# Gradient along the rows on one core: part of one early load moved to a second queue, and the waits set by hand

## The chip, the core and the metric

One of the cores of a Trainium2 chip runs the kernel. The metric is device time in microseconds (us); the lower the better. The core has five engines that run side by side (TensorE, VectorE or DVE, ScalarE or ACT, GpSimd or POOL, SyncE or SP) and 16 DMA engines that move data between main memory (HBM) and the on-chip memory of 128 partitions. An engine starts a transfer by issuing it on its queue; the 16 DMA engines carry the packets.

## The reference

```python
def setup_inputs():
    return {"x": np.random.randn(8192, 8192).astype(np.float32)}

def reference(x):
    return np.gradient(x, axis=1)
```

For every row: inside, `out[j] = (x[j+1] - x[j-1]) / 2`; at the two ends, the plain difference of the two outermost values. 268.4 MB are read and as many written.

## The kernel before

The 8192 rows are cut into 32 tiles of 256 rows. A partition holds two neighbouring rows (`R = 2`), so a tile is 128 partitions x 16384 float32, that is 65536 bytes in each partition, contiguous in main memory. Tile `i` lives in slot `i % 3` (`NB = 3`) of the on-chip memory. A slot is 64 columns wider than a tile: the load writes at column 64, the results are written from column 0 on.

For each tile, in the loop over `i`:

- `load(i)` (line 52): one transfer from main memory to the slot, issued on SP's queue. It waits for the store of tile `i - 3`, which used the same slot.
- POOL takes the four end differences into the small array `ends` (line 74). It waits for the load.
- DVE does all the rest of the tile in one instruction, a custom operation that subtracts and halves (line 80). It waits for line 74.
- DVE, or POOL for `i % 5` in (1, 3) but for the last two tiles, copies the end values over the two seams of the result (line 91).
- `store(i)` (line 56): one transfer from the slot to main memory, also on SP's queue. It waits for line 91. For `i % 3 == 1` (but the last) the store is held: it is issued after the next tile's step on line 74, so once that tile has landed.

After the third tile of a round the loads of the next three tiles are issued. SP's queue so alternates: three loads, three stores, three loads, and so on, 64 transfers in all; the last round has tiles 30 and 31. The order is written by hand (`manual_schedule`). The dependencies are declared to the framework by `chain`, which names the steps that an instruction must wait for; the framework places the semaphores.

## Time and profile before

| what | us |
|---|---|
| median of 3 runs | 1247.15 (1247.09 to 1247.3) |
| the profiled execution | 1246.62 |
| its span | 1244.7 |
| DVE busy | 554.6 |
| line 80, one tile (mean of 32) | 17.224 |
| POOL busy | 8.8 |
| first load issued, after the span's start | 0.74 |
| load, from issue to landing (median) | 57.9 |
| store, from issue to landing (median) | 40.2 |

The span is what the profiler saw of the program on the core; the time of the execution is 1.9 us more. The queue that SP fills is called q1 in the profile, the one that brings instructions to the engines q14. A transfer's landing is its semaphore's last update: a transfer of 128 partitions sends one update from each of 16 DMA engines, and the landing records hold the 16 times. The packet records hold the start, the duration and the size of each packet that a DMA engine moved, without the engine's number. Instructions of the sequencer itself (issues, semaphores, branches) carry a q behind the engine: SPq.

### The profile page before, as it was taken

What the parts mean: (1) busy time and instruction counts of PE and PEld (TensorE: products, weight loads), DVE (VectorE), ACT (ScalarE), POOL (GpSimd) and SP (SyncE); (2) the same over time, 40 slices, a digit from 0 to 9 for tenths busy, and PEclk for the clock granted to TensorE, in tenths of its full rate; (3) what the DMA queues carried; (4) which work ended last, traced back from release to release, by engine and by line L of the source; (5) the groups of instructions that cost most, each with busy time, mean ns of one, the idle gap of its engine ahead of it and who ended that gap; (6) DMA issues with size and microseconds to landing.
All of it is one profiled execution on the core that took longest, in us unless ns stands there. A gap on an engine that the chain in (4) does not pass through costs nothing.

```text
span 1244.7 us, 237 instructions
## 1 busy us (share of the span) xinstructions
DVE 554.6 (45%) x52; POOL 8.8 (1%) x48
## 2 busy tenths in 40 slices
DVE  2850582079009702850582079009603840591082
POOL 0000000000000000000000000000000000000000
DMA  9999999999999999999999999999999999999999
GB/s 404 438 436 423 421 438 438 438 438 428 432 430 430 438 438 438 423 436 436 430 434 436 438 428 432 438 436 434 425 436 434 432 436 436 436 434 430 434 409 404
DMA packets 9217, 536.88 MB, mean 431 GB/s; under 512 B 1024, under 2 KB 1024, under 8 KB 1024
## 3 DMA queue, kind: packets, MB, share of 16 engines
q1 hardware_dynamic: 9216, 536.88, 99.8%
q14 instruction: 1, 0.01, 0.0%
HBM read 268.44 MB, written 268.44 MB: 431 GB/s over the span
## 4 chain that ended last, share of the span: by engine, by line
another core or an unknown queue 74%; DVE 18%; DMA 3%; issue 2%; POOL 1%; SPq 0%; POOLq 0%
DVE slot L80 18%; DMA slot<-in_x_dram 3%; POOL ends L74 0%; POOL slot L91 0%; SPq L52 0%; POOLq L128 0%; DVE slot L91 0%
## 5 line engine op out<-in xcount | busy, mean ns | idle before, releaser
L80 DVE CUSTOM_DVE_ANT_0 slot<-slot 128x16382 f32<-128x16382 f32 x32 | 551.2, 17224 | 667.6 <-POOL ends L74 667.6
L74 POOL TENSOR_TENSOR ends<-slot 128x4 f32<-128x4 f32 x32 | 6.3, 198 | 988.5 <-DMA slot<-in_x_dram 988.5
L91 POOL COPY slot<-ends 128x4 f32<-128x4 f32 x12 | 2.3, 190 | 207.9 <-DVE slot L80 207.9
L91 DVE COPY slot<-ends 128x4 f32<-128x4 f32 x20 | 3.4, 172 | 0.7
L117 POOL MEMSET const-bfloat16-1.0<- 128x1 bf16 x1 | 0.1, 101 | 0.0
L117 POOL MEMSET const-uint8-127<- 128x1 uint8 x1 | 0.1, 101 | 0.0
L117 POOL MEMSET const-float32-0.0<- 128x1 f32 x1 | 0.1, 98 | 0.2 <-issue 0.2
L117 POOL MEMSET const-float32-1.0<- 128x1 f32 x1 | 0.1, 98 | 0.0
## 6 DMA issues: line engine op xcount, KB each, us to landing
slot<-in_x_dram SPq DMA_DIRECT2D x32, 57.9
out_dram<-slot SPq DMA_DIRECT2D x32, 40.2
```

What stands on the lines that cost most here:

```text
L74: ins = nc.gpsimd.tensor_sub(out=ends[:, i, :, :], in0=xin[:, :, 1 : m : m - 2], in1=xin[:, :, 0 : m - 1 : m - 2],)
L80: ins = nc.vector._custom_dve(dve_ops.TENSOR_TENSOR_REDUCE_SUB_MAX, out=b[:, 1 : W - 1], in0=b[:, SH + 2 : SH + W], in1=b[:, SH : SH + W - 2],
L91: ins = placer.tensor_copy(out=res[:, :, 0 : m : m - 1], in_=ends[:, i, :, :])
L117: nc = _bacc.Bacc("TRN2", target_bir_lowering=False, num_devices=1)
```

## The change

The last 960 of tile 2's 16384 columns (3840 of 65536 bytes in each partition) are no longer in SP's load of this tile. They are loaded by 15 transfers on ACT's queue, which the kernel did not use: of 15 partitions, of 14, and so on down to 2, and one of 9, from partition 127 downwards; together 128. All other loads and all stores are as before.

For this the framework's dependencies are given up: the whole loop stands in a critical section, and semaphores are allocated and waited for by hand. `landed[k]` counts 16 for each transfer into slot `k`, so tile 2 waits for 16 transfers; `stored[k]` counts the stores from the slot; `taken`, `halved` and `placed` count the three compute steps. At the end SP waits for the last store from each slot. The compute instructions, their engines and their order are the same, and so is SP's order of loads and stores.

```diff
+    SPLIT = 2
+    REST = 960
+    RANGES = (15, 14, 13, 12, 11, 10, 9, 8, 7, 6, 5, 4, 3, 2, 9)
...
-    def load(i):
-        b = slots[i % NB]
-        ins = nc.sync.dma_start(out=b[:, SH : SH + W], in_=x_sets[i])
-        loads.append(chain(i, ins, *([stores[i - NB]] if i >= NB else [])))
...
+    with tc.tile_critical():
+        landed = [tc.alloc_semaphore(f"landed{k}") for k in range(NB)]
...
+        def load(i):
+            k = i % NB
+            b = slots[k]
+            at = W - REST if i == SPLIT else W
+            if i >= NB:
+                nc.sync.wait_ge(stored[k], home[i - NB])
+            nc.sync.dma_start(out=b[:, SH : SH + at], in_=x_sets[i][:, 0:at]).then_inc(landed[k], 16)
+            n_landed[k] += 16
+            if i == SPLIT:
+                lo = P
+                for rows in RANGES:
+                    lo, hi = lo - rows, lo
+                    nc.scalar.dma_start(
+                        out=b[lo:hi, SH + at : SH + W], in_=x_sets[i][lo:hi, at:W]
+                    ).then_inc(landed[k], 16)
+                    n_landed[k] += 16
+            arrived[i] = n_landed[k]
...
+        def store(i):
+            k = i % NB
+            eng, count = done[i]
+            nc.sync.wait_ge(placed[eng], count)
+            nc.sync.dma_start(out=out_sets[i], in_=slots[k][:, 0:W]).then_inc(stored[k], 16)
+            n_stored[k] += 16
+            home[i] = n_stored[k]
...
+            nc.gpsimd.wait_ge(landed[k], arrived[i])
+            nc.gpsimd.tensor_sub(
...
+            ).then_inc(taken, 1)
+            nc.vector.wait_ge(taken, i + 1)
...
+            ).then_inc(halved, 1)
...
+            eng.wait_ge(halved, i + 1)
...
             if held is not None:
-                store(*held, at[0])
+                nc.sync.wait_ge(taken, i + 1)
+                store(held)
                 held = None
...
+        for k in range(NB):
+            nc.sync.wait_ge(stored[k], n_stored[k])
```

More of the change, by code (lines that the diff above doesn't have):

```diff
@@ L35 @@
     slots = [pool.tile([P, SH + W], f32, name=f"slot{k}", tag=f"slot{k}") for k in range(NB)]
-    loads, stores = [], [None] * nsets
-    in_front = {}
-    def chain(i, ins, *needed):
-        group, engine = f"slot{i % NB}", ins.ins.engine
-        keep = [o.ins for o in needed]
-        if in_front.get(engine, (None,))[0] == group:
-            keep.append(in_front[engine][1])
-        tc.declare_no_dep(ins.ins, group=group, keep=keep, reason="implied by the needed step")
-        tc.add_to_no_dep_group(group, ins.ins)
-        in_front[engine] = group, ins.ins
-        return ins
@@ L50, in load @@
-    def load(i):
-        b = slots[i % NB]
-        ins = nc.sync.dma_start(out=b[:, SH : SH + W], in_=x_sets[i])
-        loads.append(chain(i, ins, *([stores[i - NB]] if i >= NB else [])))
-    def store(i, done, later):
-        ins = nc.sync.dma_start(out=out_sets[i], in_=slots[i % NB][:, 0:W])
-        stores[i] = chain(i, ins, done)
-        if later is not None:
-            tc.add_manual_dep(
-                ins.ins,
-                later.ins.name,
-                mybir.DependencyInfo(mybir.DependencyClass.Sync, mybir.DependencyReason.DATA),
-                reason="issued once the next tile has landed",
-            )
@@ L66 @@
-    held = None
-    with tc.manual_schedule():
+    with tc.tile_critical():
+        landed = [tc.alloc_semaphore(f"landed{k}") for k in range(NB)]
+        stored = [tc.alloc_semaphore(f"stored{k}") for k in range(NB)]
+        taken = tc.alloc_semaphore("taken")
+        halved = tc.alloc_semaphore("halved")
+        placed = {nc.vector: tc.alloc_semaphore("placed_v"), nc.gpsimd: tc.alloc_semaphore("placed_g")}
+        n_landed, n_stored = [0] * NB, [0] * NB
+        n_placed = {nc.vector: 0, nc.gpsimd: 0}
+        arrived, home, done = [0] * nsets, [0] * nsets, [None] * nsets
+        def load(i):
[22 more added lines that the diff above has]
+            home[i] = n_stored[k]
@@ L68 @@
         for i in range(NB):
             load(i)
+        held = None
         for i in range(nsets):
-            b = slots[i % NB]
+            k = i % NB
+            b = slots[k]
             xin = b[:, SH : SH + W].rearrange("p (t m) -> p t m", m=m)
-            ins = nc.gpsimd.tensor_sub(
+            res = b[:, 0:W].rearrange("p (t m) -> p t m", m=m)
+            nc.gpsimd.wait_ge(landed[k], arrived[i])
+            nc.gpsimd.tensor_sub(
                 out=ends[:, i, :, :],
@@ L77 @@
                 in1=xin[:, :, 0 : m - 1 : m - 2],
-            )
-            at = [chain(i, ins, loads[i])]
-            ins = nc.vector._custom_dve(
+            ).then_inc(taken, 1)
+            nc.vector.wait_ge(taken, i + 1)
+            nc.vector._custom_dve(
                 dve_ops.TENSOR_TENSOR_REDUCE_SUB_MAX,
@@ L86 @@
                 s1=0.5,
-            )
-            halved = chain(i, ins, *at)
-            res = b[:, 0:W].rearrange("p (t m) -> p t m", m=m)
-            placer = nc.gpsimd if i % 5 in (1, 3) and i < nsets - 2 else nc.vector
-            ins = placer.tensor_copy(out=res[:, :, 0 : m : m - 1], in_=ends[:, i, :, :])
-            placed = chain(i, ins, halved)
+            ).then_inc(halved, 1)
+            eng = nc.gpsimd if i % 5 in (1, 3) and i < nsets - 2 else nc.vector
+            eng.wait_ge(halved, i + 1)
+            eng.tensor_copy(out=res[:, :, 0 : m : m - 1], in_=ends[:, i, :, :]).then_inc(placed[eng], 1)
+            n_placed[eng] += 1
+            done[i] = eng, n_placed[eng]
             if held is not None:
-                store(*held, at[0])
+                nc.sync.wait_ge(taken, i + 1)
+                store(held)
                 held = None
             if i % NB == 1 and i + 1 < nsets:
-                held = i, placed
+                held = i
             else:
-                store(i, placed, None)
+                store(i)
             if i % NB == NB - 1:
-                for k in range(i + 1, min(i + 1 + NB, nsets)):
-                    load(k)
+                for j in range(i + 1, min(i + 1 + NB, nsets)):
+                    load(j)
+        for k in range(NB):
+            nc.sync.wait_ge(stored[k], n_stored[k])
 _INS = ['x']
```

## The prediction

> **What bounds the kernel now.** I read the page first: what is busy, and the DMA queues.

> ```profile
> span 1244.7 us, 237 instructions
> ...
> DVE 554.6 (45%) x52; POOL 8.8 (1%) x48
> ...
> q1 hardware_dynamic: 9216, 536.88, 99.8%
> q14 instruction: 1, 0.01, 0.0%
> ...
> slot<-in_x_dram SPq DMA_DIRECT2D x32, 57.9
> out_dram<-slot SPq DMA_DIRECT2D x32, 40.2
> ```

> The compute engines are idle more than half the time; SP's queue q1 keeps the 16 DMA engines busy for 99.8% of the span. Next, the DMA share by stage (columns: stretch, its length, DVE busy, POOL busy, PE clock, DMA share, GB/s).

> ```profile
> 0.00:1.70 1.70, 0.00 (x0) 0.20 (x4) 1.00 0.00 0
> ...
> 62.00:1202.00 1140.00, 501.04 (x46) 7.83 (x40) 1.00 1.00 433
> 1202.00:1205.00 3.00, 1.54 (x2) 0.00 (x0) 1.00 0.87 371
> ```

> The queue never runs dry before 1202 us. The timeline shows why the 13% idle after it does not matter:

> ```profile
> 1185.91 0.20 POOL L74 TENSOR_TENSOR ends<-slot 128x4 f32<-128x4 f32 x1 [77.09 <-DMA slot<-in_x_dram]
> 1186.14 17.23 DVE L80 CUSTOM_DVE_ANT_0 slot<-slot 128x16382 f32<-128x16382 f32 x1 [59.86 <-POOL ends L74]
> 1203.40 0.17 DVE L91 COPY slot<-ends 128x4 f32<-128x4 f32 x1
> 1203.60 19.65 SPq L56 DMA_DIRECT2D out_dram<-slot  x2
> 1205.22 0.20 POOL L74 TENSOR_TENSOR ends<-slot 128x4 f32<-128x4 f32 x1 [19.11 <-DMA slot<-in_x_dram]
> ```

> Store 30 is issued at 1203.60 and its first packets start at 1204.5. The first DMA engine had finished load 31 at 1202.24 and waits; the last finished at 1205.15 and never waits. So the end is set by **the slowest of the 16 DMA engines**: its 512 packets, back to back.

> So I read the packet records one by one (start, duration, size). A packet is one row of 65536 bytes; it belongs to the engine whose packet before ended within 8 ns of its start. This gives 16 rows of 512 packets (one record is missing); the engines' numbers are not in the records. 7778 of 8192 packets take 2418 ns. I call "lag" how far an engine is behind an unbroken row of packets, 2.415 us apart, from 1.75 us on. Mean over the engines of what is added, in us:

> ```
> starts of the first packet (0 to 1.20 late)        0.25
> first packet longer than 2.418                      0.55
> tiles 0-1, rest                                     0.02
> load 2 (two thirds or more in its last packet)      1.16
> rounds 1-9, loads to stores: .06 .45 .07 .33 .21 .08 .35 .02 .02 = 1.59
> lag before store 30: mean 3.54, least 2.30, most 5.05
> ```

> The extra of a round sits almost wholly in the last load packet before the stores begin. The first time, at 58 us, all engines reach it within 0.65 us and lose 0.84 to 1.12 us each. The rounds that follow lose 0.06 to 0.45 while the engines are 0.6 to 2.0 us apart, and 0.02 once they are 2.6 us apart, which is more than one packet. The order is not smooth (.06 at 0.6 us apart), so this is a tendency, no law. Landings agree: 0.62 us between first and last engine at load 0, 2.92 at load 31.

> **The change, part by part.** The profiled execution took 1246.62 us (1.9 around its span), 0.53 under the median 1247.15; I add differences to the median.

> *Waits by hand.* Loads and stores keep their order on SP; POOL, DVE and the held stores wait for the same steps. One wait costs SP 17 ns (its EVENT_SEMAPHORE rows) and lies behind a full queue: nothing, up to 0.1 us at store 30 if it is exposed.

> *Entry and exit of the critical section.* Each engine gets one more branch, and SP a step in which it waits for the others and releases them. The trace has such handshakes at the end:

> ```profile
> L128 SPq EVENT_SEMAPHORE  x7: 17/28/28, 1223.3 to 1244.6; - x7
> L128 POOLq EVENT_SEMAPHORE  x4: 17/17/17, 1244.0 to 1244.6; - x4
> ```

> From the last landing, 1243.85, to 1244.67 there are two: about 0.4 each. One more before the first load and one after the last landing lie bare on the path: 2 x 0.35 = **+0.7** (0 if they share the old ones, 1.6 at twice that).

> *Fifteen issues on ACT.* SP's issue of a load takes 340 ns (median of 32); 15 make 5.1 us on an engine that does nothing else. Hidden: their data is wanted by tile 2, which lands at 62 us. If ACT held back SP's first load, the cost were one issue, 0.34. Tile 0 lands later by the pieces that slip in between its rows, 15 x 0.3 = 4.5 us at most; store 0 is then issued at 45 instead of 40.4, still ahead of its turn at 58.

> *Bytes moved between engines.* SP's load of tile 2 loses 3840 of 65536 bytes per row: 8 rows x 0.142 us (3840/65536 x 2.418) = 1.14 us less on every engine. The pieces come back on ACT's queue. How they spread is not in this trace: evenly would be 8 each and no shift. All on one engine is 128 x 0.151 = 19 us. I take one row an engine, counted from the same engine each time, since a row is the packet here. Then the fifteen transfers put 15 pieces on the first engine, 15, 14, 13 and so on, none on the last.

> [...]

> *Price of a piece.* Low end: 0.142 plus a 4-byte semaphore packet of 9 ns = 0.151. High end: the only packet of another ring under load (q14, 8192 bytes, 997.06 us) took 309 ns, and the q1 packet behind it on that engine 2579 instead of 2418, so 161 ns more: 0.312. That row is the nearest, but it came alone and unannounced, while the pieces stand queued; I take 0.205, a third of the way. The first engine then has 15 x 0.205 - 1.14 = **+1.94** (+1.13 to +3.54), the last -1.14.

> *What the shift does at the load-store turns.* The engines are now some 3.1 us apart (15 steps of 0.205) before the first turn, which the trace shows as nearly free (0.02). Of the 2.7 us lost from load 2 on I leave 0.9 for the slowest engine (0.2 if the turns are clean; all of it if spread is not the reason).

> Sum for the slowest: 0.25 + 0.55 + 0.05 + 1.94 + 0.9 = 3.7 against 5.05, so -1.35; with +0.7: -0.65, **1246.5 us**.

> **The rivals.**

> A, *faster*: clean turns and cheap pieces. 0.85 + 1.13 + 0.2 = 2.2, against 5.05: -2.85, handshakes +0.3: **1244.6**. For it: 15 steps of 0.151 fill 2.27 us, nearly one packet, so that one engine turns at a time. Against: rounds at 2.0 us apart still lost 0.35.

> B, *slower*: the switch between rings costs the full 161 ns each time. The first engine gets +3.54. Were its lag average before, it ends at 3.54 + 3.54 = 7.1, 2.0 past the old slowest, +0.7: **1249.9**; were it the slowest already, 1251.4. It decides once a piece costs over (5.05 - 3.54 + 1.14)/15 = 0.177 and the turns stay as dear. For it: the q14 row. Against: with spread the turns should get cheaper, which gives back up to 1.8.

> C, *only the handshakes*: the engines that get more bytes had slack (2.30 against 5.05), those that decide are little changed, the turns too: +0.7, **1247.9**. Against: the turns cost more than half the lag, and the shift reaches every engine before them.

> [...]

> D, *the pieces pile up* on one engine: +18 and more, **1265**.

> **How the numbers follow.** Forecast 0.42 (its own range 1245.2 to 1247.8), A 0.23, B 0.18, C 0.13, D and the unforeseen 0.04. A measurement of this kernel tells about 0.2%, 2.5 us: faster means under 1244.7, slower over 1249.6. A and a stray part of the forecast make faster 0.25; B and D 0.21; the rest, 0.54, is the same. Range 1244.2 to 1249.9: A's time with its bare handshakes, up to B's nearer end.

> **What would show it.** Entry: the first load's issue later than 0.74 us by some 0.35; exit: more than 0.82 us from last landing to end. Pieces: fifteen packets of 3840 bytes on one engine, fourteen on others, none on one, all before 40 us, and q1 packets of 2418 or some 2580 behind them. Turns: the packets at 58 us at 2.5 instead of 3.3 us. Spread at load 31 (2.92): about 3 if the shift stays, with the last landing of load 31 near 1204.5. I am wrong if the packets at 58 us stay at 3.3 though the engines are 2 us apart, or if pieces cost 0.3 and more.

## The result, and the profile after

The changed kernel takes 1249.61 us (median of 16 runs, 1248.88 to 1250.11), the kernel before 1247.12 (median of 16, 1246.46 to 1247.52): a ratio of 1.0020, interval 1.0013 to 1.0027. It is slower, by 2.5 us. The profiled execution took 1250.04 us, 3.42 more than that of before; 0.9 of this is that the one lies 0.43 above its median and the other 0.50 below, so the parts below are worth a little less in the median.

From the page of the changed kernel: the span, what is busy, the DMA queues. q10 is ACT's queue.

```profile
span 1248.1 us, 243 instructions
...
DVE 554.6 (44%) x52; POOL 8.8 (1%) x48
...
q1 hardware_dynamic: 9216, 536.38, 99.5%
q10 hardware_dynamic: 256, 0.49, 0.1%
q14 instruction: 1, 0.01, 0.0%
```

The engines do the same work, the DMA engines are as busy as before, and the same 537 MB are moved. The 256 packets of q10 are 128 pieces of 3840 bytes and 128 semaphore updates of 4 bytes. Now the start, in the timeline of the changed kernel (start, duration, engine, line, what; in brackets the idle time before it and what ended it).

```profile
0.91 6.08 ACTq L62 DMA_DIRECT2D slot<-in_x_dram  x15
0.95 1.33 SPq L56 DMA_DIRECT2D slot<-in_x_dram  x3
25.72 0.20 POOL L86 TENSOR_TENSOR ends<-slot 128x4 f32<-128x4 f32 x1 [25.28 <-DMA slot<-in_x_dram]
...
47.11 0.20 POOL L86 TENSOR_TENSOR ends<-slot 128x4 f32<-128x4 f32 x1 [21.20 <-DMA slot<-in_x_dram]
```

POOL's first step on a tile follows the tile's landing at once (tile 1 lands at 47.05, the step starts at 47.11). Here are the same two steps of the kernel before:

```profile
22.69 0.20 POOL L74 TENSOR_TENSOR ends<-slot 128x4 f32<-128x4 f32 x1 [22.25 <-DMA slot<-in_x_dram]
...
41.99 0.20 POOL L74 TENSOR_TENSOR ends<-slot 128x4 f32<-128x4 f32 x1 [19.10 <-DMA slot<-in_x_dram]
```

Tile 0 is there 3.0 us later, tile 1 5.1 us later. The view by stretches says where the bandwidth went (columns as before: stretch, length, DVE, POOL, PE clock, DMA share, GB/s). First the changed kernel, then the one before.

```profile
4.00:42.00 38.00, 16.05 (x1) 0.20 (x1) 1.00 0.99 396
```
```profile
4.00:42.00 38.00, 17.40 (x2) 0.21 (x2) 1.00 1.02 442
```

The DMA engines are busy all the time in both (share 0.99 and 1.02), and move a tenth less in the changed kernel (396 against 442 GB/s): the packets take longer. The packet records show which. These are the rows of the engine that carries no piece at all, start in us and duration in ns:

```
after, engine without pieces:  5.39 2434   7.82 2824   10.64 2714   13.35 3012   16.36 2418   18.77 2807   21.57 2418
                               23.99 2611  26.60 2702  29.30 2418   31.71 2666   34.38 2418   36.79 2682   39.47 2418
before, any engine:            2418 to 2420 for nearly every row of tiles 0 and 1 after the first
```

Its rows are stretched by 0.15 to 0.6 us whenever the others carry pieces, and take about 2418 in between. So the cost falls on all 16 engines, whoever carries the piece: of the 256 full rows that start before 45 us, 166 are stretched by more than 0.02 us, against 25 of 288 in the kernel before.

Why only every second row, the engine with all fifteen pieces shows (p is a piece, s its semaphore update of 4 bytes, K a row; start in us, duration in ns):

```
32.21:p149 32.35:K2651 35.00:s9 35.01:K2422 37.43:p149 37.57:K2675 40.24:s9 40.25:K2422 42.67:p149 42.81:K2805
```

A piece and its update each take a turn of their own between two rows. Fifteen pieces so stretch over some 28 rows: the last one starts at 67.60 us, where the prediction had all of them before 40 us, and POOL's step on tile 2 starts at 70.71 us instead of 62.37. The rows of SP's queue do not wait for that: store 0 still occupies the DMA engines then, and their share is 1.01 from 60 to 70 us and 0.99 from 70 to 90.

The end, from the sequencer's rows of the critical section (duration min/median/max, first and last start):

```profile
L40 SPq COMPARE_BRANCH  x1: 38/38/38, 1246.7 to 1246.7; - x1
...
L40 SPq NOP  x2: 13/16/18, 0.7 to 1247.2; - x2
```

The last store lands at 1246.26, SP leaves the section at 1246.7 and has all engines together at 1247.2; only then come the handshakes that the kernel before has too, up to 1248.05. From the last landing to the end it is 1.79 us, against 0.83.

The sum of the packets, in us and as a mean over the engines down to "all later extra" (the last landing is that of the slowest engine), with the prediction's way of counting (extra over 2.418 for 65536 bytes, in proportion for 61696):

```
                                before   after
first packet starts at            2.00    2.26
first row, extra                  0.55    0.18
rows of loads 0 to 2, extra       0.22    3.19
pieces, less the 1.14 saved          -    0.72
turn at 58 (61) us, extra         0.96    0.16
all later extra                   1.66    0.89
last landing                   1243.85 1246.26
from there to the end of the span 0.83    1.79
```

3.0 us are lost beside the pieces and 1.6 gained back at the turns; 0.7 is lost in the pieces themselves and 0.3 at the start, which the first row gives back. That is +2.0 in the mean (the landings of load 30 say +1.97), and the slowest engine now lies 2.20 behind the mean at load 30 (before: 1.70): +2.41 at the last landing. The section's exit adds 0.96.

### The profile page after: what moved, and what is told of

It reads as the page before. It is cut to its first block, busy times and chain, and to the rows that moved or that the text cites. A ratio compares the mean times of both kernels' runs of the same rounds, so it can differ in the third digit from the quotient of the medians.

```text
span 1248.1 us, 243 instructions
## 1 busy us (share of the span) xinstructions
DVE 554.6 (44%) x52; POOL 8.8 (1%) x48
## 2 busy tenths in 40 slices
DMA packets 9473, 536.88 MB, mean 430 GB/s; under 512 B 1152, under 2 KB 1152, under 8 KB 1280
## 3 DMA queue, kind: packets, MB, share of 16 engines
q1 hardware_dynamic: 9216, 536.38, 99.5%
## 4 chain that ended last, share of the span: by engine, by line
another core or an unknown queue 76%; DVE 18%; DMA 4%; POOL 1%; issue 0%; SPq 0%
DVE slot L92 18%; DMA slot<-in_x_dram 4%; POOL ends L86 1%; POOL slot L102 0%; SPq L56 0%; DVE slot L102 0%; SPq L143 0%; SPq L40 0%
## 6 DMA issues: line engine op xcount, KB each, us to landing
out_dram<-slot SPq DMA_DIRECT2D x32, 40.2
slot<-in_x_dram SPq DMA_DIRECT2D x31, 57.9
```

## The experiments

Each is a variation of the changed kernel or of the one before, run beside the kernel before on the same chip. Ratios are to that kernel. The table of the packets' extra follows after the last one.

### The section alone

```diff
-    REST = 960
-    RANGES = (15, 14, 13, 12, 11, 10, 9, 8, 7, 6, 5, 4, 3, 2, 9)
+    REST = 0
+    RANGES = ()
```

> The critical section with its hand-placed semaphores, but no pieces: tile 2 is loaded whole on SP's queue. Theory (the section's entry and exit cost 0.2 and 1.0 us, the pieces the rest): +1.2 us against the kernel before, packets of the first two loads at 2418 ns, the turn at 58 us at 3.3 us again. Rival (the section costs all of it): +2.5 us.

1248.27 us, ratio 1.0009 (1.0000 to 1.0018): +1.05 against 1247.22. The first load is issued at 0.95 instead of 0.74 us; from the last landing to the end it takes 1.69 us. Rows of tiles 0 and 1 keep 2418 ns, the turn costs 0.97 us. So the section explains 1.05 of the 2.5, and the pieces some 1.4.

### One transfer, evenly spread

```diff
-    RANGES = (15, 14, 13, 12, 11, 10, 9, 8, 7, 6, 5, 4, 3, 2, 9)
+    RANGES = (128,)
```

> The same 960 columns of tile 2 on ACT's queue, but as one transfer of 128 partitions: 8 pieces on every engine, no shift between engines. Theory R (a piece of another queue between SP's rows is what slows the rows): the rows of the first two loads are slow again, some 0.2 to 0.4 us for each round of pieces, 8 x 0.3 = 2.4 us, and +1.2 for the section, +3.6 us against before, and the turn at 58 us as dear as before. Theory F (a row is slowed because the pieces of 15 or fewer partitions are written to partitions that other engines write to): rows at 2418 ns, +1.2 us.

1248.29 us, ratio 1.0010 (1.0001 to 1.0019): the same as the section alone. In its timeline the tiles land 19.3 us apart (43.51 - 24.20), as in the kernel before:

```profile
0.91 0.39 ACTq L62 DMA_DIRECT2D slot<-in_x_dram  x1
...
24.20 0.20 POOL L86 TENSOR_TENSOR ends<-slot 128x4 f32<-128x4 f32 x1 [23.75 <-DMA slot<-in_x_dram]
```

One engine's packets in order show a piece (p) between rows (K) of the other queue:

```
2.99:p149  3.13:K2418  5.55:p149  5.69:K2418  8.11:p149  8.25:K2418  10.67:p149  10.81:K2418  13.23:p149  13.37:K2418
```

Changing between the two queues costs nothing here; the piece takes 149 ns and the row behind it 2418. Theory R falls, and with it rival B's mechanism.

### The pieces behind tile 2's load, on SP's queue

```diff
-                    nc.scalar.dma_start(
+                    nc.sync.dma_start(
```

> The same 15 transfers, issued on SP's queue behind tile 2's load, so that no piece comes between rows of tiles 0 and 1. Theory R: rows of loads 0 to 2 at nominal duration, pieces at 0.15 us each, the shift between engines is there before the first turn, which costs 0.2 instead of 0.96 us in the mean; the slowest engine 1.8 us ahead of the kernel before, the section +1.2: -0.6 us. Theory F: the pieces slow each other, but only over some 2 us: about the same, -0.4. Rival (the shift does not relieve the turns): +2.3 us.

1247.29 us, ratio 1.0001 (0.9992 to 1.0010): +0.07 against the kernel before, 0.98 under the section alone, 2.3 under the changed kernel. The rows of tiles 0 and 1 keep 2418. The pieces, now one behind the other at 60 us, take some 150 to 884 ns, and tile 2 is there at 64.75 instead of 62.37 us. The turn costs 0.60, all that is later 0.61. The same bytes in the same fifteen transfers thus cost 2.3 us less when no rows are beside them. Not all of that comes from the packets: in the profiled executions it takes 1.31 us from the last landing to the end, against 1.69 with the section alone and 1.79 in the changed kernel, and the last landing is 0.27 us earlier than with the section alone. The turns do become cheaper, but more than half of what this kernel gains on the section alone lies in the exit; why the exit is shorter was not found. The forecast of -0.6 was missed by 0.7, within the interval.

### Eight transfers of sixteen neighbours

```diff
-    RANGES = (15, 14, 13, 12, 11, 10, 9, 8, 7, 6, 5, 4, 3, 2, 9)
+    RANGES = (16,) * 8
```

> The 960 columns on ACT's queue in 8 transfers of 16 neighbouring partitions: again 8 pieces on every engine and no shift, but now each transfer's 16 pieces go to 16 neighbouring partitions. Theory R: as with the one even transfer, +3.6 us. Theory F: rows slow as in the changed kernel, 0.3 us and more in each of 8 rounds, +3.6 us, while the one even transfer is at +1.2.

1250.34 us, ratio 1.0029 (1.0017 to 1.0040). The tiles land 21.0 us apart:

```profile
26.35 0.20 POOL L86 TENSOR_TENSOR ends<-slot 128x4 f32<-128x4 f32 x1 [25.91 <-DMA slot<-in_x_dram]
47.35 0.20 POOL L86 TENSOR_TENSOR ends<-slot 128x4 f32<-128x4 f32 x1 [20.80 <-DMA slot<-in_x_dram]
```

Eight pieces on each engine as in the even transfer, no shift, yet most of the stretched rows take 2.53 to 2.92 us, and 3.1 us are lost on each engine. What costs is neither the shift nor the second queue. What differs is how the partitions are grouped: 16 neighbours to a transfer, or all 128 in one; in which partitions the pieces of one moment lie in the even transfer, the records do not show. (There are also eight transfers now instead of one; the last pair of kernels keeps their number the same.)

### Writing side or reading side

Both use eight transfers of 16 again, with 16 neighbours on one side and every eighth partition on the other. The edit of the first is shown; the second swaps the two patterns.

```diff
+                for j in range(8):
+                    nc.scalar.dma_start(
+                        out=b[16 * j : 16 * j + 16, SH + at : SH + W], in_=x_sets[i][j:P:8, at:W]
+                    ).then_inc(landed[k], 16)
```

> As the eight transfers of 16 on ACT's queue, but each reads 16 rows of main memory that lie 8 partitions' rows apart (512 KB) and writes 16 neighbouring partitions; the 960 columns of tile 2 so end in other partitions than the reference has them in. Theory FW (neighbouring partitions are what is crowded, on the writing side): rows beside the pieces at 2.7 to 3.0 us as before, 3.1 us a DMA engine in all, +3 us against the kernel before. Theory FR (neighbouring rows of main memory are crowded, on the reading side): rows at 2418 ns, +1.1 us.

> The mirror image: each of the eight transfers reads 16 neighbouring rows of main memory and writes every eighth partition; again the 960 columns of tile 2 end in other partitions. Theory FW: rows at 2418 ns, +1.1 us against the kernel before. Theory FR: rows at 2.7 to 3.0 us, +3 us.

Writing to neighbours, reading far apart: 1253.82 us, ratio 1.0050 (1.0030 to 1.0070), four runs between 1250.22 and 1256.63; rows of loads 0 to 2 2.78 us slower an engine. Writing far apart, reading neighbours: 1249.05, ratio 1.0023 (1.0011 to 1.0035), ten runs between 1248.10 and 1255.77; 1.29 us, the stretched rows 0.15 longer in the median. So it is mainly the writing side. Neither theory had the second half right: writing to every eighth partition still costs a part. The last pair of kernels bears on that. The times scatter more than those of any other kernel; why was not found.

### The counts of the change, partitions eight apart

```diff
+    RANGES = ((15, 1), (14, 2), (13, 3), (12, 4), (11, 5), (10, 6), (9, 7), (8, 8))
...
+                        at_rows = slice(j + 8 * lo, j + 8 * (lo + rows - 1) + 1, 8)
```

> The changed kernel on ACT's queue with nearly the same counts per transfer (15 and 1, 14 and 2, down to 8 and 8), but the partitions of a transfer lie 8 apart, in main memory and on the chip. Theory F, either side: rows of loads 0 and 1 at 2418 ns; relief of the turns stays; as the fifteen transfers on SP: within 0.5 us of the kernel before, 2 us under the changed kernel. Rival (the unequal counts or the number of transfers slow the rows): +2.5 us, as the changed kernel.

1249.68 us, ratio 1.0021 (1.0012 to 1.0031). The profiled execution is the fastest of its ten, 1248.11; in it the rows of loads 0 to 2 lose 1.80 us instead of 3.19, 0.10 to 0.17 in most rounds. The profile shows the cost halved; the median shows no gain. The prediction of this run missed, and what the slower executions lose their time in was not seen.

### Four transfers on SP's queue, without the section

```diff
 (kernel before)
+    RANGES = (56, 40, 24, 8)
...
+                piece = nc.sync.dma_start(out=b[lo:hi, SH + at : SH + W], in_=x_sets[i][lo:hi, at:W])
+                loads[i].append(chain(i, piece))
```

The last 960 columns of tile 2 come in four transfers on SP's queue behind its load.

> [...] If the shift relieves the turns and the section costs 1.05 (the section alone measured that): as the fifteen transfers on SP less the section, -1.0 us against the kernel before. Rival (relief needs fifteen even steps): no change, or up to +0.7 from the shift itself.

1247.30 us, ratio 1.0000 (0.9991 to 1.0008). The turn at 58 us costs 0.65, all later 1.58 (before: 0.96 and 1.66); the rival with no change is right. It was meant to be faster than both kernels, and is not.

### Every fourth partition, and eight neighbours

Sixteen transfers of 8 partitions each, with `lo, step = 32 * (j // 4) + j % 4, 4` in the first and `8 * j, 1` in the second:

```diff
+                for j in range(16):
+                    lo, step = 32 * (j // 4) + j % 4, 4
+                    rows = slice(lo, lo + 7 * step + 1, step)
+                    nc.scalar.dma_start(
+                        out=b[rows, SH + at : SH + W], in_=x_sets[i][rows, at:W]
+                    ).then_inc(landed[k], 16)
```

> The 960 columns of tile 2 on ACT's queue in 16 transfers of 8 partitions that lie 4 apart (0, 4, ... 28 and so on). [...] If any 16 rounds of pieces from few engines slow the rows: +3 us and more.

> [...] By the same count a round costs 3 x 0.15 = 0.45 us: rows beside the pieces at 2.8 to 2.9 us in the 16 rounds that carry pieces, some 5 to 7 us on the engines that carry them; +4 to +7 us against the kernel before. [...] Open: whether the 8 engines without pieces keep rows of 2418 ns.

Every fourth: 1247.96 us, ratio 1.0007 (0.9998 to 1.0016). Eight neighbours: 1248.99, ratio 1.0017 (1.0008 to 1.0027). The stretch from 4 to 42 us, every fourth first:

```profile
4.00:42.00 38.00, 17.39 (x2) 0.20 (x1) 1.00 1.00 433
```
```profile
4.00:42.00 38.00, 17.11 (x1) 0.20 (x1) 1.00 1.00 413
```

And rows of an engine without pieces in each, in ns, one after the other:

```
every fourth:      2420 2418 2420 2418 2420 2418 2418 2418 2418 2418 2418 2418 2418
eight neighbours:  2467 2418 2593 2418 2731 2418 2661 2625 2418 2546 2418 2700 2418
```

The same number of pieces on the same number of engines at the same moments: harmless to the rows of tiles 0 and 1 when a round's pieces are four partitions apart, 0.05 to 0.34 us for everyone when they are neighbours. In this run only loads pay this: the last two rounds of the eight neighbours, at 67 and 72 us, fall beside rows of store 0, and all 46 rows that start from 66 us until these pieces are through stay within 3 ns of 2418. So in this run the price falls on rows that are written into the on-chip memory, as the pieces are, which agrees with the two kernels on the writing side (2.78 us for writing to neighbours, 1.29 for reading them). And not all of it ends in the time: beside neighbours the rows of loads 0 to 2 lose 2.6 us more, the turns after them 2.2 us less (table below), and the two medians lie 1.0 us apart. For every fourth partition +1 us (0 to +2.2) was forecast, and +0.89 came. For the eight neighbours the size was put too high: +1.92 us instead of 4 to 7. No run shows the 3 x 0.15 us of its forecast; the stretched rows of tiles 0 and 1 lost 0.23 us in the median, and most rounds less than 0.45. Also seen: with every fourth partition, the rows of tile 2 itself lose 0.15 us beside each round after 46 us; why was not found.

The packets' extra in all profiled executions (mean over the engines, us):

```
                              loads 0-2   turn   later   median against before
before                             0.22   0.96   1.66        -
after                              3.19   0.16   0.89     +2.49
section alone                      0.02   0.97   1.15     +1.05
one even transfer                  0.05   0.73   1.96     +1.07
pieces on SP                       0.14   0.60   0.61     +0.07
eight of sixteen neighbours        3.13   0.00   0.95     +3.12
write near, read far               2.78   0.00   3.04     +6.62
write far, read near               1.29   0.00   0.82     +1.85
counts of the change, 8 apart      1.80   0.23   0.86     +2.48
four on SP, no section             0.29   0.65   1.58     +0.10
every fourth                       0.33   0.52   2.22     +0.89
eight neighbours                   2.97   0.37   0.13     +1.92
```

## Why the prediction was wrong

**The bound** held: the 16 DMA engines set the end before and after, q1 is busy 99.5% of the span, and the compute steps are the same to 0.1 us.

**The step that failed** is "Price of a piece", and with it the line that let the pieces "slip in between its rows" as a delay of their own length only. Two ends were named, 0.151 for the piece and its semaphore, and 0.312 with the change of queue; 0.205 was taken. The change of queue costs nothing: 149 ns, and 2418 behind it, in the even transfer. What costs is that a transfer's pieces, all written at about the same moment (the fifteen of the first transfer start between 1.94 and 2.65 us), go to neighbouring partitions, and that the rows of all 16 engines take longer with them, 3.19 us for loads 0 to 2 in the mean. The prediction counted bytes for each DMA engine, and never asked to which partitions those bytes go and who else writes there. On the engine without pieces it expected a gain of 1.14 and rows of 2418; its rows of loads 0 and 1 alone lost 2.8 us.

The size goes with how the partitions of a transfer lie, by the rows of tiles 0 and 1 that are stretched by more than 0.02 us: the median of these loses 0.36 us with sixteen neighbours, 0.23 with eight, 0.14 to 0.15 with sixteen that lie eight apart, and with eight that lie four apart only 2 of 240 rows are stretched at all. What in the on-chip memory makes the distance count is not shown. Nor do the runs show why the rows of an engine that carries no piece are stretched too; that stays open.

**Rival B** gave 1249.9 and 1249.61 came, but for another reason. Its mechanism, the change between queues, is refuted, and a piece's own 0.149 us lies below the 0.177 from which B was to decide. That its number came close is luck.

**Entry and exit**: +0.7 was taken, between 0 and 1.6. The section alone measured 1.05, with the entry cheaper (0.21) and the exit dearer (0.86 in the section alone, 0.96 in the changed kernel; 0.48 with the pieces on SP) than the 0.35 each.

**Which engine gets how many pieces**: the fifteen pieces of the sum, 15 x 0.205, and the engine with none were the author's assumption, which no run had shown before. In the records of the changed kernel one engine has all fifteen and one has no piece, as taken. In the transfers of 8, eight engines carry about 16 each and eight none. Which engines these are, records without engine numbers do not show.

**The turns**: right in their effect here, 0.16 instead of 0.96 for the first and 0.89 instead of 1.66 for the rest, 1.6 us in the mean; the prediction expected to keep 0.9 on the slowest engine. But spread is not the whole reason. With transfers of 16 the first turn is free (0.00) though the engines are only 0.6 to 1.1 us apart; the four transfers on SP put the engines 2.25 us apart before the second turn and gain nothing later; and the profiled executions without shift and without crowded pieces (before, the section alone, the even transfer) scatter between 1.15 and 1.96 in the later turns. What a turn costs, and why, stays open.

**Issue on ACT**: right. Fifteen issues took 6.08 us instead of 5.1, beside everything. Tile 2 was complete 8.3 us later than before, mostly because each update takes a turn too (fifteen pieces over some 28 rows); the DMA engines had other rows to carry meanwhile. **Waits by hand**: right, nothing in the middle of the kernel. **The slowest engine**: expected 1.35 us earlier, it was 2.4 later at the last landing (the engines were 3.54 us apart at load 31, so the shift stayed, as forecast); 3.0 us beside the pieces outweigh what the turns gave back.

**Rival C**, by which only the handshakes are paid, is what the even transfer shows (+1.07); the change itself is worse for the shape of its transfers.

## What to carry to other kernels

When a transfer is cut by partitions, ask where a round's packets go, and not only how many bytes each DMA engine has: packets that several engines write at once to neighbouring partitions slowed the rows of all 16 here while they were loading, by 2.78 to 3.19 us an engine over loads 0 to 2. The cut by columns over all 128 partitions (+1.07) and the partitions four apart (+0.89) cost about what the section alone does (+1.05): these are the two to try. And in this kernel, at 99.8% DMA, a critical section with one handshake more at each end cost 1.05 us, and none of these shifts brought back more than that.
